# Three edits to a two-block layer stack on one core: an instruction of the second block tied to its place, parameter loads one step ahead, rotation tables later

## The chip, the cores and the metric

The kernel runs on one core of a Trainium2 chip. The metric is the device time of one execution in microseconds (us), the median over runs; the profile shows one execution, whose span (first to last instruction) is a little shorter than its time. Engines are named as the profile names them: PE (TensorE), DVE (VectorE), ACT (ScalarE), POOL (GpSimd) and SP (SyncE, which here only issues DMAs; SPq is its queue).

## The reference

Everything is float32, one sequence of 512 tokens of width 2048. Two blocks follow one another, each of two layers with adaptive modulation (shift, scale and gate from a vector c).

```python
def first_block(x, c, positions, ...):
    cos, sin = rope_tables(positions)
    for l in range(2):
        mod = silu(c) @ w_ada[l] + b_ada[l]          # shift, scale, gate
        h = rms_norm(x, norm_g[l]) * (1 + scale) + shift
        u, z, q, k, v = split(h @ w_in[l])
        y_ssm = s5_mixer(u, a, b, c, ...)            # state recurrence, 64 groups x 64 states
        y_att = diff_attention(rope(q), rope(k), v, lam)   # 8 heads, softmax - lam * softmax
        x = x + gate * (concat(y_ssm, y_att) * silu(z)) @ w_out[l]
    return rms_norm(x, final_g)

def second_block(x, c, ...):                         # gated delta rule beside sliding window attention
    beta = sigmoid(ba[..., 0:8])
    g = -exp(a_log) * softplus(ba[..., 8:16] + dt_bias)
    ...
```

## The kernel before

**Products.** Weights come from HBM as 128x1024 pieces. `piece()` (L255 to L272) loads one into a tile `raw` (L265, four buffers), ACT rounds it to `hi` (L266, three buffers), DVE writes the rest `lo = raw - hi` (L267, three buffers). Every product is made of three matmuls, hi with the rounded activations HH, hi with their rest HL, and lo with HH: L279, L280 and L282 for feature-major outputs (`mm3`), L352 to L354 for the token-major v. PE works through them in the order written.

**The ada weights** (w_ada) are streamed beside the rest: `ada_piece` loads one into a buffer of the same `raw` pool (L530) and DVE makes a dot product of it (L516). All loads go out on SP's queue, in order.

**Layers.** `layer` (L1011) runs the first block's two layers: the projections, then eight attention heads; beside these it takes steps of the state recurrence from the generator `ssm_steps` (L784). That prepares 64 chunk states in G, then runs 62 steps of three instructions on POOL (L812 to L814), written at a lower priority (`self.later(600)`). Each step multiplies by the table `A8[l]`. Then for eight groups it copies the states with four DMAs from G to a tile `s` (L830), each group's tile being one buffer, and multiplies them (L835, L837).

**The parameters** of the recurrence come from a generator `ssm_params` (L573), in quarters: `prep(qd)` loads a quarter of B and C (a DMA into a tile `rp`, three buffers) and makes their powers with DVE and POOL (L658 to L660). `par` is this generator for layer 0; `late()` in `build` takes its first step behind ssm_pad, rope_tables, lambdas and gain_root. rope_tables uses G's slots 0 to 3 as scratch; the first quarter uses 0 to 3 too.

**misc** is a tile of 128x640 with several uses: columns 0 to 127 hold A8 of layer 0, 128 to 255 that of layer 1, 384 to 511 the recurrence's scratch. In the second block `gates2` (L1138) takes 32-column slots of it by name; the fourth, `al`, is columns 96 to 127. `al` is written by one DVE instruction (L244) from `rep`, which holds a_log since the program's start.

**What sets the order.** The tile framework schedules the program itself. It takes the instructions by priority (the order in which they are written, unless changed) as soon as its own model sees their inputs and buffers ready, and so fixes one order for each engine and for each queue; the waits between engines follow from tiles read and written. An instruction whose inputs are there early can be placed far ahead of its neighbours in the source. At run time every engine takes its list strictly in order.

Of the kernel before, what the change touches and what calls it, by code (L numbers as in the profile page):

```python
# [11 lines left out]
I32 = mybir.dt.int32  # L12
# [156 lines left out]
class Kern:  # L169
# [282 lines left out]
    def rope_tables(self):  # L452
        nc = self.nc
        self.cosT, self.sinT = self.tab[:, :S], self.tab[:, S:]
        pi = self.G[:, 0, :].bitcast(I32)
        pf, r, w = (self.G[:, i, :] for i in (1, 2, 3))
        pos = self.I["pos"]
        nc.sync.dma_start(pi, bass.AP(tensor=pos.tensor, offset=pos.offset, ap=[[0, 128], [1, S]]))
        nc.vector.tensor_copy(pf, pi)
        self.ts(pf, pf, self.v("inv_freq"))  # L460
        self.reduce_angle(r, pf, w)
        lim = 3.1415925
        self.ts(r, r, -lim, lim, MAX, MIN)
        self.act(self.sinT, r, AF.Sin)
        self.ts(self.sinT, self.sinT, self.v("rope_sign"))
        self.act(w, r, AF.Sin, scale=0.5)
        self.tt(w, w, w, MUL)
        self.ts(self.cosT, w, -2.0, 1.0)
# [104 lines left out]
    def ssm_params(self, l):  # L573
# [5 lines left out]
        i = nc.sync.dma_start(ssa, I[f"ssa{l}"])  # L579
# [5 lines left out]
        def tmp(n, dt=F32):  # L585
            if n not in names:
                names[n] = cur[0]
                cur[0] += 32
            t = g[:, names[n]:names[n] + 32]
            return t if dt == F32 else t.bitcast(dt)  # L590
# [6 lines left out]
        step, x, th, e, em1, r, w2 = (tmp(k) for k in ("step", "x_", "th", "e", "em1", "rr", "w2"))  # L597
# [55 lines left out]
        def powmul(T, tm, out, f, src, n, qd, op=ADD):  # L653

            fv = f.rearrange("p (k r a) -> p k r a", k=2, r=2)[:, :, :, qd * 8:qd * 8 + 8]
            for r in range(2):
                t = tm[r][:, :8 * n].rearrange("p (a c) -> p a c", a=8)
                T(t, fv[:, 1, r].unsqueeze(2).to_broadcast([128, 8, n]), src[:, 1 - r], MUL)  # L658
                T(out[:, r], fv[:, 0, r].unsqueeze(2).to_broadcast([128, 8, n]), src[:, r], MUL)  # L659
                T(out[:, r], out[:, r], t, op)  # L660

        def prep(qd):
            sbq = self.t2("rp", 3).rearrange("p (k r a c) -> p k r a c", k=2, r=2, a=8)
            nc.sync.dma_start(sbq.rearrange("p k r a c -> p (k r) (a c)"),
                              I[f"ssb{l}"].rearrange("p (k q c) -> p k q c", k=4, q=4)[:, :, qd])
            tv = self.t2("n", 3), self.t2("n", 3)
            E = self.G[:, 4 * (qd % 2):4 * (qd % 2) + 4, :].rearrange("p a b -> p (a b)").rearrange("p (r a dc) -> p r a dc", r=2, a=8)
            powmul(V, tv, E[:, :, :, 0:16], cf, sbq[:, 0], 16, qd)
            for i, n in enumerate((16, 32, 64)):
                powmul(V, tv, E[:, :, :, n:2 * n], pw[i], E[:, :, :, 0:n], n, qd)  # L670

            nc.gpsimd.tensor_scalar(sbq[:, 1, 1], sbq[:, 1, 1], -1.0, None, MUL)

            Cb = self.t2("p", 4).rearrange("p (r a h c) -> p r a h c", r=2, a=8, h=2)
            nc.gpsimd.memset(Cb, 0.0)
            for h in range(2):
                rows = slice(64 * h, 64 * h + 64)
                nc.gpsimd.tensor_copy(Cb[rows, :, :, h, :], sbq[rows, 1])
            return E, Cb, sbq

        def products(E, Cb):
            kp = self.sbank("sc", 2)
            for x in range(2):
                for r in range(2):
                    for j in range(4):
                        a = 4 * x + j
                        nc.tensor.matmul(kp[32 * j:32 * j + 32, 128 * x:128 * x + 128], Cb[:, r, a].rearrange("p h c -> p (h c)"),
                                         E[:, r, a], start=r == 0, stop=r == 1)
            k2 = self.t2("p", 4)
            nc.scalar.copy(k2[:, :256], kp[:, :256])  # L690
            return kp, k2
# [18 lines left out]
        def turned(qd, E, rs):  # L710

            for r in rs:
                for a0 in range(0, 8, 4):
                    tp = self.sbank("tr", 2)
                    for a in range(4):
                        nc.tensor.transpose(tp[:, a * 128:(a + 1) * 128], E[:, r, a0 + a], self.ident)
                    ft = self.t2("p", 4)
                    nc.scalar.copy(ft, tp)
                    nc.sync.dma_start(self.FT_d[l][qd * 2 + a0 // 4, r], ft)

        def carried(qd, sbq):
# [7 lines left out]
            for r in range(2):  # L729
                for h in range(2):  # L730
                    nc.sync.dma_start(self.CA_d[l][qd][64 * r:64 * r + 64, h], CA[64 * h:64 * h + 64, r])
        made = prep(0)
        yield
        for qd in range(4):
            E, Cb, sbq = made
            k = products(E, Cb)
            turned(qd, E, (0,))
            yield
            turned(qd, E, (1,))
            lags(qd, *k)  # L740
            yield
            if qd < 3:
                made = prep(qd + 1)
            carried(qd, sbq)
            yield
            yield
# [394 lines left out]
    def gates2(self):  # L1141

        nc = self.nc
        ba = self.ba.rearrange("p (t c) -> p t c", c=16)
        used = {}

        def sm(name, dt=F32):
            i = used.setdefault(name, len(used))
            t = self.misc[:, 32 * i:32 * i + 32]
            return t if dt == F32 else t.bitcast(dt)  # L1150
        v3 = lambda t: t.rearrange("p (t h) -> p t h", h=8)
        x, e, y, al = sm("x"), sm("e"), sm("y"), sm("al")
        self.beta, self.nbeta, gc = sm("beta"), sm("nbeta"), sm("gc")

        self.ts(v3(x), ba[:, :, 0:8], -1.0)
        self.exp_acc(x, sm, e)
        self.ts(e, e, 1.0, None, ADD)
        nc.vector.reciprocal(self.beta, e)
        self.ts(self.nbeta, self.beta, -1.0)

        dt = self.rep[:, 8:16].unsqueeze(1).to_broadcast([128, 4, 8])
        self.tt(v3(x), ba[:, :, 8:16], dt, ADD)
        self.ts(y, x, -1.0)
        self.tt(y, y, x, MIN)
        self.exp_acc(y, sm, e)
        self.ts(y, e, 2.0, None, ADD)
        nc.vector.reciprocal(y, y)
        self.tt(e, e, y, MUL)
        self.tt(y, e, e, MUL)
        acc = sm("acc")  # L1170
        self.ts(acc, y, 2.0 / 17, 2.0 / 15)
        for k in (13, 11, 9, 7, 5, 3, 1):
            self.tt(acc, acc, y, MUL)
            self.ts(acc, acc, 2.0 / k, None, ADD)
        self.tt(acc, acc, e, MUL)
        self.stt(acc, x, 0.0, acc, MAX, ADD)
        self.ts(v3(al), self.rep[:, 0:8].unsqueeze(1).to_broadcast([128, 4, 8]), 1.0)
        self.exp_acc(al, sm, e)
        self.stt(acc, acc, -1.0, e, MUL, MUL)
        ps = self.sbank("sc", 2)  # L1180
        nc.tensor.matmul(ps[:, :32], self.tri, acc, start=True, stop=True)
        nc.vector.tensor_copy(gc, ps[:, :32])
        self.gc = gc

        ps = self.sbank("sc", 2)
        nc.tensor.transpose(ps[:32, :128], gc, self.ident)
        gt = self.t2("n", 3)[:32, :128]
        nc.vector.tensor_copy(gt, ps[:32, :128])
        self.g_d = self.dp.tile([32, 128], F32, name="g_d")
        nc.sync.dma_start(self.g_d, gt)  # L1190

        ps = self.sbank("sc", 2)
        nc.tensor.matmul(ps[:, :32], self.sellast, gc, start=True, stop=True)
        self.bg, self.kd, self.egl = sm("bg"), sm("kd"), self.misc[:, 512:544]
        assert len(used) <= 16
        self.exp_acc(gc, sm, self.bg)
        self.tt(self.bg, self.bg, self.beta, MUL)
        self.tt(x, ps[:, :32], gc, SUB)
        self.exp_acc(x, sm, self.kd)
        nc.vector.tensor_copy(e, ps[:, :32])  # L1200
        self.exp_acc(e, sm, self.egl)
# [403 lines left out]
def build(ctx, tc, I, O):  # L1605
    K = Kern(ctx, tc, I, O)
# [9 lines left out]
    for m in range(KT):  # L1616
        x, t = K.A[:, m, :], K.t2("n", 3)
# [11 lines left out]

    def late():  # L1630
        K.ssm_pad()
        K.rope_tables()
        K.lambdas()
        K.gain_root()
        next(par)
    K.start(K.acts(), before, late)
    xs = K.dp.tile([2, KT, 128, 512], F32, name="xs")


# [82 lines left out]
```

## Time and profile before

| | |
|---|---|
| runs shown | 3535.65, 3535.91, 3533.48 us |
| median | 3535.65 us |
| profiled execution | 3532.28 us |
| its span | 3530.5 us, mean granted TensorE clock 0.974 |
| PE busy | 3324.8 us (94% of the span) |
| DVE, ACT, POOL busy | 2190.3 (62%), 1217.0 (34%), 570.4 (16%) |
| DMA | 565.02 MB moved, mean 160 GB/s |

Shares are of the whole span; the stages differ. POOL is busy in two stretches only, once for each layer of the first block. A wait for several things is put down to the one that came last.

### The profile page before, as it was taken

Reading aid. Unit: us, or ns where it says so; the run is one execution under the profiler, and the core shown is the slowest. Engines: PE = TensorE matmul, PEld = TensorE weight load, DVE = VectorE, ACT = ScalarE, POOL = GpSimd, SP = SyncE. Lnnn points to the kernel's source line nnn. Section 1 sums busy time; section 2 is a strip of 40 time slices with the busy share of each in tenths; the row PEclk is TensorE's granted clock in tenths of the full one; section 3 lists DMA queues with packets and bytes.
Section 4 is the critical chain, followed back from the end, with each engine's and each line's share of the span. In section 5 each row is a group of like instructions: output and inputs, shape, how many; then the busy total and the mean of one; then the engine's idle time right before and its main releaser. Section 6 shows DMA issues by size and latency. Waiting matters only on the chain.

```text
span 3530.5 us, 45193 instructions
## 1 busy us (share of the span) xinstructions
PE 3324.8 (94%) x16541; PEld 2714.8 (77%) x16541; DVE 2190.3 (62%) x4244; ACT 1217.0 (34%) x2107; POOL 570.4 (16%) x732
## 2 busy tenths in 40 slices
PE   6988879999999888989999999999999999999999
PEld 4866657878888667777787887788888877788887
DVE  7993766767559736866665588933893266534432
ACT  3422433353233223333443344222532244433311
POOL 0073480000116605800001202000210000000000
PEclk8999989999999999999999999999999999999999
DMA  9857535757766775456567636333333332234442
GB/s 330 297 150 183 183 106 173 212 157 240 225 197 197 235 193 181 128 168 193 159 214 228 210 122 134 104 110 99 99 101 108 96 99 77 73 99 142 142 140 99
DMA packets 262813, 565.02 MB, mean 160 GB/s; under 512 B 74428, under 2 KB 111549, under 8 KB 262589
## 3 DMA queue, kind: packets, MB, share of 16 engines
q1 hardware_dynamic: 262590, 562.13, 52.2%
q8 instruction: 130, 2.13, 0.3%
q14 instruction: 93, 0.76, 0.1%
HBM read 497.89 MB, written 50.50 MB: 155 GB/s over the span
## 4 chain that ended last, share of the span: by engine, by line
PE 60%; DMA 12%; DVE 12%; POOL 8%; issue 4%; SPq 2%; ACT 2%; DVEq 0%; ACTq 0%; POOLq 0%
PE pp L280 17%; PE pp L279 17%; PE pp L282 17%; DMA raw<-in_wada 6%; DVE lo L267 3%; POOL misc L812 2%; DVE raw L516 2%; DMA raw<-in_win 2%; POOL G L814 2%; POOL misc L813 2%; DVE G L249 1%; POOL G L660 1%; DMA FT_d<-p 1%; POOL G L659 1%; DMA raw<-in_w 1%
## 5 line engine op out<-in xcount | busy, mean ns | idle before, releaser
L279 PE MATMUL pp<-HH,hi 128*128 128x512 f32 (+1 forms) x3568 | 1388.0, 392 | 40.5 <-ACT HH L566 20.7
L280 PE MATMUL pp<-HL,hi 128*128 128x512 f32 (+1 forms) x3440 | 1332.4, 391 | 1.5 <-DVE HL L252 1.5
L266 ACT CAST hi<-raw 128x1024 fp32r<-128x1024 f32 (+1 forms) x538 | 559.9, 1042 | 1142.9 <-PE pp L280 851.4
L282 PE MATMUL pp<-HH,lo 128*128 128x512 f32 (+1 forms) x3568 | 894.3, 388 | 0.1
L267 DVE TENSOR_TENSOR lo<-raw,hi 128x1024 fp32r<-128x1024 f32 (+1 forms) x538 | 668.9, 1245 | 359.2 <-PE pp L282 178.4
L279 PEld LDWEIGHTS pp<-HH,hi 128*128 128x128 f32 x3568 | 677.9, 190 | 184.2 <-ACT HH L566 22.3
L282 PEld LDWEIGHTS pp<-HH,lo 128*128 128x128 f32 x3568 | 656.8, 188 | 136.9 <-issue 6.3
L280 PEld LDWEIGHTS pp<-HL,hi 128*128 128x128 f32 x3440 | 653.0, 190 | 136.1 <-issue 7.0
L516 DVE CUSTOM_DVE_ANT_0 raw<-raw,cs,mod 128x1024 f32<-128x1024 f32 x112 | 148.2, 1324 | 235.4 <-DMA raw<-in_wada 235.2
L516 DVE CUSTOM_DVE_ANT_0 raw<-raw,cs,vec 128x1024 f32<-128x1024 f32 x112 | 151.6, 1353 | 167.3 <-DMA raw<-in_wada 167.1
L1676 POOL TENSOR_TENSOR rp<-rp,n 128x512 f32<-128x512 f32 (+1 forms) x43 | 59.9, 1406 | 994.1 <-ACT n L1675 581.4
L217 ACT ACTIVATE p<-p,st 128x128 f32<-128x128 f32 (+2 forms) x192 | 102.0, 531 | 258.1 <-DVE st L244 257.8
L812 POOL TENSOR_TENSOR misc<-misc,G 128x128 f32<-128x128 f32 x124 | 92.6, 747 | 237.9 <-ACT G L804 228.3
L352 PE MATMUL pp<-hi,HH 128*128 128x512 f32 (+1 forms) x320 | 121.9, 386 | 4.9 <-ACT HH L566 3.1
L353 PE MATMUL pp<-lo,HH 128*128 128x512 f32 (+1 forms) x320 | 120.7, 381 | 3.1 <-DVE lo L267 3.1
L354 PE MATMUL pp<-hi,HL 128*128 128x512 f32 (+1 forms) x320 | 116.1, 384 | 1.0 <-DVE HL L252 1.0
L280 PE MATMUL pp<-A,hi 128*128 128x512 f32 x256 | 100.7, 393 | 0.0
L660 POOL TENSOR_TENSOR G<-G,wt 128x128 f32<-128x128 f32 (+2 forms) x64 | 75.7, 1197 | 1.0
L217 ACT ACTIVATE n<-n 128x512 f32<-128x512 f32 x68 | 42.9, 631 | 94.2 <-DVE n L246 93.4
L352 PEld LDWEIGHTS pp<-hi,HH 128*128 128x128 f32 x320 | 62.5, 195 | 16.7 <-ACT HH L566 3.9
L936 PE MATMUL sc<-kh,q 128*128 128x128 f32 (+3 forms) x128 | 46.7, 367 | 28.2 <-DVE st L939 17.4
L814 POOL TENSOR_TENSOR G<-G,misc 128x64 f32<-128x64 f32 x124 | 71.2, 574 | 9.7
(332 smaller groups left out, 3924.6 us busy)
## 6 DMA issues: line engine op xcount, KB each, us to landing
raw<-in_wada SPq DMA_DIRECT2D x224, 512.0 KB, 4.1
raw<-in_w SPq DMA_DIRECT2D x164, 512.0 KB, 3.8
raw<-in_win SPq DMA_DIRECT2D x128, 512.0 KB, 4.6
raw<-in_wo SPq DMA_DIRECT2D x80, 512.0 KB, 4.6
G<-in_wad SPq DMA_DIRECT2D x64, 512.0 KB, 5.9
raw<-in_wv SPq DMA_DIRECT2D x32, 512.0 KB, 4.3
raw<-in_wglu SPq DMA_DIRECT2D x32, 512.0 KB, 4.4
raw<-in_wuA SPq DMA_DIRECT2D x18, 512.0 KB, 4.3
```

The lines of the kernel that those rows point to most:

```text
L217: i = self.nc.scalar.activation(out, src, func, **kw)
L266: nc.scalar.copy(hi[:, :n].bitcast(F32R), raw[:, :n])
L267: nc.vector.tensor_tensor(lo[:, :n].bitcast(F32R), raw[:, :n], hi[:, :n], SUB)
L279: mm(out, hi[:, sl], mh, start=first, stop=False)
L280: mm(out, hi[:, sl], ml, start=False, stop=False)
L282: mm(out, lo[:, sl], mh, start=False, stop=last)
L352: mm(pss[t][:, :n], mh[:, ts], hi[:, sl], start=first, stop=False)
L353: mm(pss[t][:, :n], mh[:, ts], lo[:, sl], start=False, stop=False)
L354: mm(pss[t][:, :n], ml[:, ts], hi[:, sl], start=False, stop=last)
L516: self.nc.vector.tensor_tensor_reduce(w, w, cs, 1.0, self.vec[:, o:o + 1] if first else m, MUL, ADD, m)
L812: T(s, a8, Sv[:, :, :, c - 1].unsqueeze(1).to_broadcast([128, 2, 2, 32]), MUL)
L814: T(Sv[:, :, :, c], Sv[:, :, :, c], s[:, 0], ADD)
```

## The change

It has three parts.

1. In `gates2`, `al` gets a tile of its own from the pool of `p` tiles (four buffers) instead of columns of `misc`.
2. In `ssm_params`, `prep(qd)` is split: `load(qd)` issues the DMA of B and C, `prep(qd, sbq)` does the rest, and the load of the next quarter is written ahead of the products of this one.
3. rope_tables, lambdas and gain_root are called after `K.start(...)`, in whose `late()` the first step of the parameters now stands alone; rope's scratch moves from G's slots 0 to 3 to slots 4 to 7.

```diff
@@ rope_tables
-        pi = self.G[:, 0, :].bitcast(I32)
-        pf, r, w = (self.G[:, i, :] for i in (1, 2, 3))
+        pi = self.G[:, 4, :].bitcast(I32)
+        pf, r, w = (self.G[:, i, :] for i in (5, 6, 7))
@@ ssm_params
-        def prep(qd):
+        def load(qd):
             sbq = self.t2("rp", 3).rearrange("p (k r a c) -> p k r a c", k=2, r=2, a=8)
             nc.sync.dma_start(sbq.rearrange("p k r a c -> p (k r) (a c)"),
                               I[f"ssb{l}"].rearrange("p (k q c) -> p k q c", k=4, q=4)[:, :, qd])
+            return sbq
+
+        def prep(qd, sbq):
             tv = self.t2("n", 3), self.t2("n", 3)
...
-        made = prep(0)
+        made = prep(0, load(0))
         yield
         for qd in range(4):
             E, Cb, sbq = made
+            if qd < 3:
+                after = load(qd + 1)
             k = products(E, Cb)
...
             if qd < 3:
-                made = prep(qd + 1)
+                made = prep(qd + 1, after)
             carried(qd, sbq)
@@ gates2
-        x, e, y, al = sm("x"), sm("e"), sm("y"), sm("al")
+        x, e, y, al = sm("x"), sm("e"), sm("y"), self.t2("p", 4)[:, :32]
@@ build
     def late():
         K.ssm_pad()
-        K.rope_tables()
-        K.lambdas()
-        K.gain_root()
         next(par)
     K.start(K.acts(), before, late)
+    K.rope_tables()
+    K.lambdas()
+    K.gain_root()
```

Below L661 the changed kernel's lines stand 3 to 5 higher (L830 becomes L835, L939 L944, L943 L948, L949 L954).

How the instructions move. First place, DVE in layer 0, the end of one attention head and the start of the next (st and p are softmax sums and probabilities, n a scaled output, raw and lo weight pieces). Before:

```order
794 L244 TENSOR_SCALAR st_3886<-st_3886 128x1 [waits DVE_49]
795 L943 RECIPROCAL st_3886<-st_3886 128x2 [waits Activation_49]
796 L244 TENSOR_SCALAR misc<-rep 128x32 [waits Pool_49]
797 L252 SCALAR_TENSOR_TENSOR st_341_3659<-st_341_3659 128x4 [waits DVE_49,Activation_49]
798 L249 TENSOR_TENSOR st_3886<-st_3886,neglam 128x1 [waits DVE_49]
799 L249 TENSOR_TENSOR st_341_3659<-st_341_3659 128x4 [waits DVE_49]
800 L244 TENSOR_SCALAR p_3897<-p_3897,st_3886 128x384 [waits DVE_49]
801 L516 ISA raw_4273,mod_100<-raw_4273,cs,mod_100 128x1024 [waits DMAHW4_49]
802 L516 ISA mod_100 128x1
803 L252 SCALAR_TENSOR_TENSOR st_341_3659<-st_341_3659 128x4 [waits DVE_49]
804 L252 SCALAR_TENSOR_TENSOR p_3890<-p_3890,st_3886,p_3897 128x384 [waits DVE_49]
805 L249 TENSOR_TENSOR n_3658<-tr_3647,st_341_3659 128x512 [waits DVE_49]
```

In the changed kernel the row `misc<-rep` is gone from here. What stood behind it comes in much the same sequence up to n_3658, and further on:

```order
809 L252 SCALAR_TENSOR_TENSOR st_341_3659<-st_341_3659 128x4 [waits DVE_49]
810 L249 TENSOR_TENSOR n_3658<-tr_3647,st_341_3659 128x512 [waits DVE_49]
811 L516 ISA raw_4321,mod_100<-raw_4321,cs,mod_100 128x1024 [waits DMAHW2_49]
812 L516 ISA mod_100 128x1
813 L267 TENSOR_TENSOR lo_4239<-raw_4237,hi_4238 128x1024 [waits Activation_49]
814 L252 SCALAR_TENSOR_TENSOR A_86<-tr_3671,subg,A_86 128x512 [waits PE_49]
815 L944 ISA p_3923,st_3912<-sc_3920,cst 128x512 [waits PE_49]
816 L944 ISA st_3912 128x1
817 L244 TENSOR_SCALAR st_3912<-st_3912 128x1 [waits DVE_49]
818 L516 ISA raw_4393,mod_100<-raw_4393,cs,mod_100 128x1024 [waits DMAHW4_49]
819 L516 ISA mod_100 128x1
820 L267 TENSOR_TENSOR lo_4269<-raw_4267,hi_4268 128x1024 [waits DMAHW3_49,Activation_49]
```

The two L516 on ada weights stand on this side of lo_4239 and lo_4269; before, L516 of raw_4393 stood behind p_3916, one row after its last write.

Second place, SP's queue at the end of layer 0's recurrence (G_90 holds the states), in the changed kernel:

```order
308 L265 DMA raw_4315<-in_win 128x1024 [waits DMAHW5_49,DVE_49]
309 L835 DMA s_412_4357<-G_90 64x256 [waits Pool_49]
310 L835 DMA s_412_4357<-G_90 64x256 [waits DMAHW7_49]
311 L835 DMA s_412_4357<-G_90 64x256 [waits DMAHW0_49]
312 L835 DMA s_412_4357<-G_90 64x256 [waits DMAHW1_49]
313 L530 DMA raw_4321<-in_wada 128x1024 [waits DMAHW2_49,DVE_49]
314 L265 DMA raw_4387<-in_win 128x1024 [waits DMAHW3_49,DVE_49]
315 L530 DMA raw_4393<-in_wada 128x1024 [waits DMAHW4_49,DVE_49]
316 L265 DMA raw_4568<-in_win 128x1024 [waits DMAHW5_49,DVE_49]
```

Before, the same nine rows stand two rows higher in the same sequence (L830 for L835): nothing moved.

Third place, PE in the changed kernel, weight piece raw_4237 and the transposes of p_3916:

```order
1533 L279 MATMUL pp_4236<-HH,hi_4238 128x512 [waits Activation_49]
1534 L280 MATMUL pp_4236<-HL,hi_4238 128x512
1535 L279 MATMUL pp_4236<-HH,hi_4238 128x512
1536 L280 MATMUL pp_4236<-HL,hi_4238 128x512
1537 L279 MATMUL pp_4236<-HH,hi_4238 128x512
1538 L280 MATMUL pp_4236<-HL,hi_4238 128x512
1539 L279 MATMUL pp_4236<-HH,hi_4238 128x512
1540 L280 MATMUL pp_4236<-HL,hi_4238 128x512
1541 L279 MATMUL pp_4236<-HH,hi_4238 128x512
1542 L954 MATMUL tr_3931<-cst,p_3916 128x128 [waits DVE_49]
1543 L954 MATMUL tr_3931<-cst,p_3916 128x128 x3
1544 L280 MATMUL pp_4236<-HL,hi_4238 128x512
```

Before, these transposes (L949) stood amid the products of the piece ahead of this one, ten rows higher; now nine products on this piece stand ahead of them.

## Rows read from the trace of the kernel before

**Rows 1.** Waits of PE, whole span: who waited for what, us in total, times, longest

```profile
PE tr L967 <- DVE n L249: 20.8, 3, 19.2
```

**Rows 2.** PE's timeline: start us, us, operation, shape, count, [idle before <-releaser]

```profile
505.11 0.39 PE L352 MATMUL pp<-hi,HH 128*128 128x512 f32 x1
505.33 0.39 PE L353 MATMUL pp<-lo,HH 128*128 128x512 f32 x1
524.90 1.09 PE L967 MATMUL tr<-cst,n 128*128 128x128 f32 x4 [19.18 <-DVE n L249]
...
538.37 0.60 PE L949 MATMUL tr<-cst,p 128*128 128x128 f32 x4
...
560.24 0.44 PE L835 MATMUL sc<-A,G 128*64 128x128 f32 x4
```

**Rows 3.** DVE's timeline of the same stretch

```profile
521.33 0.18 DVE L244 TENSOR_SCALAR misc<-rep 128x32 f32<-128x32 f32 x1 [22.35 <-POOL misc L812]
...
530.88 1.28 DVE L516 CUSTOM_DVE_ANT_0 raw<-raw,cs,mod 128x1024 f32<-128x1024 f32 x1 [4.32 <-DMA raw<-in_wada]
...
533.36 1.22 DVE L267 TENSOR_TENSOR lo<-raw,hi 128x1024 fp32r<-128x1024 f32 x1
...
535.52 0.17 DVE L943 RECIPROCAL st<-st 128x2 f32<-128x2 f32 x1 [0.88 <-ACT p L217]
...
536.52 0.74 DVE L252 SCALAR_TENSOR_TENSOR p<-p,st,p 128x512 f32<-128x512 f32 x1
...
538.63 1.28 DVE L516 CUSTOM_DVE_ANT_0 raw<-raw,cs,mod 128x1024 f32<-128x1024 f32 x1 [1.36 <-DMA raw<-in_wada]
```

**Rows 4.** POOL's timeline: first step of layer 0's recurrence, step 47, its end

```profile
399.11 0.65 POOL L812 TENSOR_TENSOR misc<-misc,G 128x128 f32<-128x128 f32 x1 [93.36 <-ACT G L804]
...
499.29 0.52 POOL L812 TENSOR_TENSOR misc<-misc,G 128x128 f32<-128x128 f32 x1
...
521.77 0.36 POOL L814 TENSOR_TENSOR G<-G,misc 128x64 f32<-128x64 f32 x1
```

**Rows 5.** SP's queue (SPq): the DMA issues of the same stretch

```profile
523.57 0.33 SPq L265 DMA_DIRECT2D raw<-in_win  x1
523.95 2.44 SPq L830 DMA_DIRECT2D s<-G  x4
526.52 0.49 SPq L530 DMA_DIRECT2D raw<-in_wada  x1
...
534.61 0.33 SPq L530 DMA_DIRECT2D raw<-in_wada  x1
```

**Rows 6.** Windows: us, busy PE, PEld, DVE, ACT, POOL (x), PEclk, DMA share, GB/s

```profile
399.00:499.00 100.00, 92.25 (x443) 74.27 (x443) 86.04 (x199) 41.75 (x116) 89.16 (x138) 0.98 0.54 164
499.00:521.00 22.00, 6.72 (x30) 5.21 (x28) 0.00 (x0) 1.05 (x1) 18.40 (x47) 0.71 0.02 9
505.00:525.00 20.00, 0.82 (x5) 0.39 (x4) 3.67 (x11) 0.00 (x0) 14.32 (x36) 0.58 0.01 3
525.00:530.00 5.00, 5.00 (x17) 4.18 (x18) 1.56 (x4) 2.01 (x4) 0.00 (x0) 0.63 0.94 254
```

**Rows 7.** Timelines of POOL, SP, DVE and PE, end of layer 1's recurrence

```profile
1496.26 0.36 POOL L814 TENSOR_TENSOR G<-G,misc 128x64 f32<-128x64 f32 x1
...
1496.65 2.43 SPq L830 DMA_DIRECT2D s<-G  x4
...
1502.93 1.28 DVE L516 CUSTOM_DVE_ANT_0 raw<-raw,cs,vec 128x1024 f32<-128x1024 f32 x1 [9.85 <-DMA raw<-in_wada]
...
1505.97 0.80 PE L936 MATMUL sc<-kh,q 128*128 128x512 f32 x1 [7.27 <-DVE st L939]
```

**Rows 8.** PE's timeline, parameter stage of layer 0

```profile
194.60 0.76 PE L279 MATMUL pp<-HH,hi 128*128 128x512 f32 x1 [5.70 <-DVE n L658]
...
234.06 1.94 PE L716 MATMUL tr<-cst,G 128*128 128x128 f32 x8 [7.17 <-issue]
```

**Rows 9.** PE's timeline, the second block near gates2

```profile
2160.19 2.03 PE L1248 MATMUL sc<-G 128*128 128x128 f32 x8 [4.17 <-DVE G L249]
```


## The prediction

> **What bounds the kernel now.** I read the table of shares first: TensorE (PE) is busy 94% of the span, so only the places where PE waits can give time back. The list of waits, sorted by total, puts one wait on top [rows 1]: PE for a VectorE (DVE) result at L249, three times, one of them 19.2 us, the longest of the kernel. The timeline of PE shows where it lies [rows 2]: PE issues its last product at 505.33, stands 19.18 us and goes on at 524.90. DVE's timeline names the cause [rows 3]: the write `misc<-rep` (L244, 128x32, 0.18 us) waited 22.35 us for L812 on GpSimd (POOL). That is the write of `al` in `gates2`, an instruction of the second block which has been moved into layer 0; its 32 columns of `misc` lie in the table that the 62-step recurrence reads, so it may only run when the recurrence has read the table for the last time. POOL's timeline gives the recurrence [rows 4]: 399.11 to 521.77 + 0.36 = 522.13. All that DVE has behind that write, the n that PE needs included, stands still.
>
> Last I read the queue of SyncE (SP), since it feeds PE with weights [rows 5]. A load can only go out when its buffer is free, so SP too stood behind DVE until 523.57. Right behind that load are the four copies `s<-G`, which read what the recurrence wrote last, and all later loads follow them in the same queue.
>
> **Part 1, al leaves misc.** In the changed order (first place) DVE loses the early wait: 22.35 us of DVE and, by the plain reading, 19.18 us of PE. The granted clock was 0.58 on average in 505 to 525 and 0.63 in 525 to 530 [rows 6]: PE had been idle, fell from 2.4 to 1.2 GHz, and stayed there for a good part of its first busy stretch, so that after the restart 5 x 0.37 = 1.9 us of work was lost. So the most this part can give is 19.2 + 1.9 = 21.1 us.
>
> I do not think that it gives it. SP's order is unchanged (second place): the first `s<-G` waits for Pool, and raw_4321 (the ada weights), raw_4387 and raw_4393 are queued behind it. DVE has L516 of raw_4321 at its row 811 and L516 of raw_4393 at its row 818, both ahead of p_3916, on which PE's transposes tr_3931 wait (third place). So the wait on the recurrence goes from DVE's write to SP's copies, and I follow it from there.
>
> *What PE has in hand.* Counted in the changed order from the point where PE stopped: 4 products left of one weight piece, 24, 24, and 9 of the next before tr_3931, in all 61, and 10 transposes. Products are 505.33 - 505.11 = 0.22 to 0.23 us apart [rows 2], four transposes take 0.60 us, so 61 x 0.23 + 10 x 0.15 = 15.5 us. PE runs dry at 505.5 + 15.5 = 521.0 instead of 505.7.
>
> *When the recurrence ends.* While DVE was 86% busy (399 to 499) 46 steps took 499.29 - 399.11 = 100.2 us, 2.18 us each; with DVE idle (499 to 521, busy 0.00) the last 16 took 22.84 us, 1.43 each [rows 4, 6]. The 46 x 0.75 = 34.5 us of delay over 86 us of DVE work is 0.40 us for each us. Now DVE does, beside these 16 steps, what it did before only after its wait, 3.67 + 1.56 = 5.2 us between 505 and 530 [rows 6]. Estimate: 5.2 x 0.40 = 2.1 us later, 524.2. Ends: nothing, if the DVE work falls between POOL's instructions, and 16 x 0.75 = 12 us, if all 16 steps run at 2.18.
>
> The row shows that POOL's steps are slower while DVE works, and by how much. The Trainium skill (SBUF — State Buffer, "SBUF: two separate sides") gives a reason: DVE and GpSimd share a pair of ports as an exclusive lock, and whoever comes second waits for the other's whole instruction, when DVE reads two SBUF inputs or runs in a two-port mode. By that rule the 5.2 us could delay POOL by up to 5.2 us and not 2.1, and the sum below would be 3.1 us higher. The trace agrees with the direction; no row separates the forms.
>
> *From there to PE.* From rows 5 and 3: the copies take 526.52 - 523.95 = 2.57 us to the next issue: 526.8. From that issue to L516 on the ada weights 530.88 - 526.52 = 4.36: 531.2. L516 1.2: 532.4. lo_4239 (L267) 1.2: 533.6; that frees the buffer for raw_4393, which before went out at 534.61, just after the same L267. From its issue to its L516 538.63 - 534.61 = 4.02: 537.6. L516 1.2 and lo_4269 1.2: 540.0. The four instructions from L943 to the end of p_3916, 535.52 to 537.26, 1.7: 541.7. PE thus waits from 521.0 to 541.7, 20.7 us, for 19.2 before.
>
> *What is left after that.* Before, PE took 560.24 - 538.37 = 21.87 us from tr_3931 to the first L835 [rows 2], with 78 products; now 63 are left, 15 x 0.23 = 3.4 less: 18.4. The restart costs its 1.9 us at the half clock as before. 541.7 + 18.4 + 1.9 = 562.0, against 560.24: **+1.8 us**, with -0.3 if POOL is not slowed.
>
> Layer 1 has no such write, and shows the same queue at work already [rows 7]: the recurrence ended at 1496.62, the copies went out at 1496.65, DVE's L516 behind them waited 9.85 us for the ada load, and PE 7.27 us. That is the second price for this place.
>
> **Part 2, loads one step ahead.** In the order neither the first layer nor the second moves a load by more than a place in SP's queue: they stood early before. I cost it at nothing; below nothing is excluded for the same reason.
>
> **Part 3, rotation tables behind the first quarter.** No work is added; the rope instructions come some 8 rows later on DVE, and the reads that free PE's accumulator banks slip a few rows behind parameter work: PE's wait of 5.70 us at 194.60 [rows 8] gets longer, at most twice as long. I take zero, because the next wait, 7.17 us at 234.06, hangs on the parameter chain, whose rows keep their places, and takes up what PE loses before it. Ends: -3 and +5.7.
>
> **Second block.** The write of al, 0.18 us, is now done there, and some DVE rows of `gates2` come about 16 places later; DVE is not the bound there. PE's wait of 4.17 us at 2160.19 [rows 9] could double. I take zero, ends 0 and +4.2.
>
> **Sum.** +1.8 + 0 + 0 + 0 = +1.8 us. The profiled execution took 3532.28, 3.4 under the median of 3535.65; a difference carries over, so against the median 3537.4.
>
> **Rivals.**
> - *The new wait costs what it costs in layer 1.* PE pays 7.27 us instead of 19.18, and about the same clock: -12, so 3523.7. For it: same code, same queue. Against it: in layer 1 only one load lay between the copies and PE's operand, here two with two L516. Chance 0.24.
> - *The stall falls away whole*: -21.1, 3514.5. It needs loads that don't wait for the recurrence, or a recurrence that ends over 15 us earlier; the order shows neither. Chance 0.10.
> - *Slower: the recurrence is dragged out.* With DVE freed, the last 16 steps run at 2.18 us like the first 46, the copies and all loads come 12 us later instead of 2.1: +11.7, 3547.4. It decides from about 13 us of DVE work beside those steps; I count 5.2, but the rows behind it may slip in, and part 3's slip would add to it. The skill's port rule above pulls the same way. Chance 0.20.
> - *The change doesn't do what it says*: the early loads move nothing, which is already in the sum.
>
> **How the numbers follow.** The forecast, the stall moved and not removed, gets 0.46, with its own range 3531 to 3543 (-0.3 to +1.8, and about 5 us either way for parts 3 and the second block). The full range must leave out at most 0.2: it takes in layer 1's price with 3 us below and the dragged recurrence, and leaves out the whole gain: 3520 to 3548. Within 0.2% (7 us, about what a measurement of this kernel can tell from no change) lies the forecast: 0.46. Faster: the first two rivals, 0.34. Slower: 0.20.
>
> **What would show it.** Right, if DVE's wait before L244 is gone, PE's 19 us wait ends later (near 520 to 540) and is put down to p (L252) or an ada load, SP's first `s<-G` goes out at the recurrence's end, 522 to 526, and L516 behind it waits for DMA. The step on POOL is right if the last 16 steps take 24 to 26 us. Wrong, if PE has no wait over 8 us between 500 and 560, or if the waits between 190 and 300 differ by more than 5 us in sum.

## The result and the profile after

| | before | after |
|---|---|---|
| median | 3535.52 us (4 runs) | 3558.07 us (4 runs, 3553.67 to 3565.03) |
| ratio | 1 | 1.0063 [1.0051, 1.0075] |
| profiled execution, its span | 3532.28, 3530.5 us | 3557.99, 3556.2 us |
| mean granted clock | 0.974 | 0.970 |
| PE, DVE busy | 3324.8, 2190.3 us | 3336.7, 2200.5 us |

The change makes the kernel 22.5 us slower, outside the range of 3520 to 3548; the forecast was 3537.4. Of the span's 25.7 us, 11.9 are PE's busy time for the same 16541 instructions, at a lower clock, and 13.8 are idle time of PE.

To see where they arise I set the two traces side by side by PE's products: the time between the k-th and the m-th product of one is subtracted from that of the other, with k and m at the times of the trace of before that head the columns. (The lists are equally long.) All kernels of the study but the three with K_d on POOL's queue stand here; the runs behind the first two rows are of the same kernel.

| us against before's profile | 5–219 | 219–452 | 452–565 | 565–636 | 636–764 | 764–2122 | 2122–2951 | sum to the end |
|---|---|---|---|---|---|---|---|---|
| the change | 4.5 | 1.9 | −2.2 | 0.7 | 8.2 | 1.8 | 10.5 | 25.3 |
| the change again (e5_after) | 5.7 | −1.4 | −0.5 | 2.1 | 3.5 | −3.6 | 8.3 | 12.1 |
| part 1 alone (e2_al) | −0.4 | 2.1 | 1.3 | −0.5 | −0.3 | −5.7 | 7.2 | 5.2 |
| al in free columns of misc (e1_own) | 1.7 | 1.6 | 2.6 | 0.2 | 2.7 | 0.2 | −1.3 | 5.8 |
| al in y's columns (e9_al_y) | 1.0 | 2.6 | 1.7 | −0.1 | 1.6 | −0.4 | −0.8 | 5.3 |
| part 3 alone (e3_rope) | 4.4 | 2.0 | −1.6 | −0.1 | 10.8 | 2.4 | −3.4 | 14.0 |
| part 3 again (e17_rope) | 3.5 | 0.9 | −0.6 | −0.4 | 10.7 | 2.3 | 0.5 | 16.3 |
| part 3, scratch slots 7 to 4 (e16_rope_perm) | 3.7 | 2.0 | 2.3 | −1.6 | 1.6 | −3.4 | −2.3 | 0.5 |
| slots 4 to 7 alone (e6_slots) | 2.5 | 2.2 | 0.7 | −0.8 | 5.9 | 3.2 | −0.6 | 12.5 |
| later calls alone (e7_calls) | 14.6 | −0.1 | 0.9 | −1.5 | 2.2 | −0.9 | −0.2 | 14.5 |
| e1_own and part 3 (e8_own_rope) | 4.7 | 0.9 | −2.2 | −0.3 | 12.9 | −1.8 | −0.8 | 11.5 |
| e1_own, all `s` copies on POOL's queue (e4_own_poolq) | 2.6 | 4.9 | −21.2 | 3.3 | 7.4 | −10.1 | −3.4 | −16.3 |
| e1_own, first group's copies there (e10_own_pool0) | 0.6 | 1.3 | −21.8 | 3.8 | 9.0 | −7.7 | −0.5 | −15.7 |
| e9_al_y, all `s` copies there (e11_y_pool) | 0.5 | 2.3 | −21.0 | 2.7 | 10.0 | −6.3 | −2.0 | −15.1 |
| the change, all `s` copies there (e12_after_pool) | 3.4 | 0.6 | −20.1 | −0.1 | 2.7 | −7.2 | 7.2 | −13.8 |

These are single executions, and a row's sum can stand several us from the ratio of its medians; a stretch is read only where several kernels agree. They agree on this: the place the prediction was about, 452 to 565, is even where the copies stay on SP's queue; the loss lies ahead of 452, in 636 to 764, and in the second block. The edge at 219 cuts through a loss that is made up again: counted from 5 us, the eight kernels with part 3 or with its slots (e7_calls aside) stand 2.5 to 5.7 us behind at 219, between 2.2 ahead and 0.3 behind at 320, and 4.0 to 6.5 behind at 452. The three kernels with al alone stand 1.7 to 3.6 behind at 452.

**The place of the forecast.** PE's list of waits after, by total (who waited for what, us, times, longest):

```profile
PE pp L279 <- ACT HH L566: 20.6, 3, 10.0
PE tr L954 <- DVE A L252: 18.8, 3, 17.6
PE sc L941 <- DVE st L944: 18.2, 11, 8.7
```

The wait for n [rows 1] is gone and another of nearly its length stands there. PE's timeline, then DVE's, SP's and POOL's of the changed kernel (columns as in [rows 2]):

```profile
520.70 0.38 PE L954 MATMUL tr<-cst,p 128*128 128x128 f32 x2
538.68 0.90 PE L954 MATMUL tr<-cst,p 128*128 128x128 f32 x3 [17.60 <-DVE A L252]
```

```profile
535.53 1.28 DVE L516 CUSTOM_DVE_ANT_0 raw<-raw,cs,mod 128x1024 f32<-128x1024 f32 x1 [20.68 <-DMA raw<-in_wada]
...
537.88 0.75 DVE L252 SCALAR_TENSOR_TENSOR A<-tr,subg,A 128x512 f32<-128x512 f32 x1
```

```profile
506.12 0.33 SPq L265 DMA_DIRECT2D raw<-in_win  x1
529.24 2.43 SPq L835 DMA_DIRECT2D s<-G  x4
531.77 0.53 SPq L530 DMA_DIRECT2D raw<-in_wada  x1
```

```profile
404.63 0.72 POOL L817 TENSOR_TENSOR misc<-misc,G 128x128 f32<-128x128 f32 x1 [99.51 <-ACT G L809]
...
504.00 0.54 POOL L817 TENSOR_TENSOR misc<-misc,G 128x128 f32<-128x128 f32 x1
...
528.85 0.36 POOL L819 TENSOR_TENSOR G<-G,misc 128x64 f32<-128x64 f32 x1
```

DVE's 22.35 us behind the write of al [rows 3] have become 20.68 us behind an ada load. SP issues nothing from 506.12 to 529.24: the copies at the head of its queue wait for the recurrence, which ends at 528.85 + 0.36 = 529.21, and the ada load goes out behind them. PE loses 17.60 us for 19.18.

**636 to 764.** PE's waits there, by the trace after; before had one wait of 6.2 us for DVE instead:

```profile
PE sc L842 <- DMA s<-G: 4.9, 3, 2.3
PE sc L840 <- DMA A<-K_d: 3.7, 1, 3.7
```

```profile
PE tr L967 <- DVE G L842: 6.2, 1, 6.2
```

The windows of the same products, after and then before (columns as in [rows 6]), show 9.9 us of idle time for 6.2, and 4.8 us more of busy time at a lower clock:

```profile
640.93:777.38 136.45, 126.54 (x703) 103.67 (x702) 90.67 (x241) 47.57 (x132) 0.00 (x0) 0.95 0.61 174
```

```profile
636.27:764.24 127.97, 121.74 (x702) 99.67 (x700) 90.54 (x242) 47.76 (x132) 0.00 (x0) 0.97 0.66 188
```

**The second block.** PE's timeline and POOL's after, then POOL's before:

```profile
2185.01 0.80 PE L1131 MATMUL tr<-wt,ones 128*128 128x512 f32 x1 [4.83 <-POOL wt L1129]
```

```profile
2176.99 3.11 POOL L1249 TENSOR_TENSOR G<-G,cst 128x512 f32<-128x512 f32 x1 [1.80 <-ACT G L217]
2180.05 3.16 POOL L1250 TENSOR_TENSOR A<-A,cst 128x512 f32<-128x512 f32 x1
2183.17 1.79 POOL L1129 TENSOR_TENSOR wt<-n,wt 128x512 fp32r<-128x512 f32 x1
```

```profile
2148.63 1.66 POOL L1245 TENSOR_TENSOR A<-A,cst 128x512 f32<-128x512 f32 x1 [1.35 <-ACT A L217]
2150.25 1.28 POOL L1124 TENSOR_TENSOR wt<-n,wt 128x512 fp32r<-128x512 f32 x1
2151.49 1.30 POOL L1244 TENSOR_TENSOR G<-G,cst 128x512 f32<-128x512 f32 x1
```

Before, POOL made wt ahead of the last pair on G and A, and PE waited 0.92 us for it; now wt stands behind that pair, whose two instructions take 3.1 us each, and PE waits 4.83. This wait is not the whole loss. PE's waits here, from the list after and then from that before:

```profile
PE tr L1133 <- ACT n L1123: 7.3, 2, 3.8
PE tr L1131 <- POOL wt L1129: 7.0, 2, 4.8
...
PE sc L1253 <- DVE G L249: 0.3, 1, 0.3
```

```profile
PE tr L1128 <- ACT n L1118: 3.8, 1, 3.8
...
PE tr L1126 <- POOL wt L1124: 0.9, 1, 0.9
```

PE now waits twice for wt and twice for n, while the wait of 4.17 us for G [rows 9] is gone. Between 2122 and 2334 this makes 3.9 us more idle time and 2.6 us more busy time; the second wait for n, near 2883, adds 3.5. POOL does not stand idle in the second block, as the remark on its two busy stretches may suggest: between 2122 and 2334 it is busy for 28.0 us before and for 37.1 us after.

### The profile page after: what moved, and what is told of

Same layout as the page of the kernel before. It is cut to its first block, busy times and chain, and to the rows that moved or that the text cites. A ratio compares the mean times of both kernels' runs of the same rounds, so it can differ in the third digit from the quotient of the medians.

```text
span 3556.2 us, 45179 instructions
## 1 busy us (share of the span) xinstructions
PE 3336.7 (94%) x16541; PEld 2722.1 (77%) x16541; DVE 2200.5 (62%) x4244; ACT 1217.4 (34%) x2107; POOL 573.1 (16%) x732
## 5 line engine op out<-in xcount | busy, mean ns | idle before, releaser
L279 PE MATMUL pp<-HH,hi 128*128 128x512 f32 (+1 forms) x3568 | 1392.5, 394 | 45.9 <-ACT HH L566 20.6
L516 DVE CUSTOM_DVE_ANT_0 raw<-raw,cs,mod 128x1024 f32<-128x1024 f32 x112 | 147.4, 1316 | 258.8 <-DMA raw<-in_wada 258.7
L516 DVE CUSTOM_DVE_ANT_0 raw<-raw,cs,vec 128x1024 f32<-128x1024 f32 x112 | 150.0, 1339 | 157.2 <-DMA raw<-in_wada 156.9
L352 PE MATMUL pp<-hi,HH 128*128 128x512 f32 (+1 forms) x320 | 122.3, 387 | 14.6 <-DVE A L249 11.5
L353 PEld LDWEIGHTS pp<-lo,HH 128*128 128x128 f32 x320 | 62.6, 196 | 13.0 <-DVE lo L267 3.2
```

What stands on the lines that cost most here:

```text
L279: mm(out, hi[:, sl], mh, start=first, stop=False)
L352: mm(pss[t][:, :n], mh[:, ts], hi[:, sl], start=first, stop=False)
L353: mm(pss[t][:, :n], mh[:, ts], lo[:, sl], start=False, stop=False)
L516: self.nc.vector.tensor_tensor_reduce(w, w, cs, 1.0, self.vec[:, o:o + 1] if first else m, MUL, ADD, m)
```

## The experiments

### Where al lies: e1_own, e2_al, e9_al_y

```diff
-        x, e, y, al = sm("x"), sm("e"), sm("y"), sm("al")
+        ... al = columns 544:576 of misc, which are free      # e1_own
+        ... al = self.t2("p", 4)[:, :32]                      # e2_al, part 1 alone
+        ... al = y's columns                                  # e9_al_y
```

> Kernel before with one edit: al lies in 32 free columns of misc (544 to 575) that no other step reads, so DVE writes it at the start of the program and waits for nothing; all else is ordered as before. Theory 1 (the wait of layer 0 passes from DVE to the copies s<-G in SP's queue, and costs PE the same): 3533 to 3539 us, a wait of PE of 15 to 21 us that begins near 519 to 521. Theory 2 (the freed DVE drags out the recurrence, and that is the loss of the changed kernel): 3543 to 3550. Plain reading (the wait goes away): 3513 to 3517.

> Kernel before with part 1 alone, as the change has it (al in a p tile, written in the second block). The order differs from before in layer 0 by the one row, and in the second block in some thousand rows. Theory 1 (loss by rows that moved): as the run with al in free columns up to 2150 us, then 7 to 11 us lost in the second block, 3541 to 3549. Theory 2 (loss in layer 0): slower by 8 to 13 before 600 us, nothing in the second block. If the second block's loss belongs to parts 2 or 3: 3533 to 3539.

> Part 1 done another way: al written over y, which gates2 has read for the last time just before; tied to its place, but no p tile is held. Only 112 rows on DVE stand otherwise than before; PE, ACT, POOL and SP are ordered as before. Theory 1 (the second block's loss, some 9 us between 2122 and 2951, comes of the order that the held p tile makes): none of it, 3532 to 3539, as al in free columns. Rival (writing al late costs there by itself): 4 us or more lost between 2122 and 2334.

Measured: e1_own 1.0012 [0.9999, 1.0024], e2_al 1.0019 [1.0009, 1.0029], e9_al_y 0.9998 [0.9987, 1.001]. In all three the wait on the recurrence is there, on the same transposes as after the change (PE's timelines of e1_own, e2_al and e9_al_y):

```profile
537.55 0.90 PE L949 MATMUL tr<-cst,p 128*128 128x128 f32 x3 [22.72 <-DVE A L252]
```

```profile
535.41 0.90 PE L949 MATMUL tr<-cst,p 128*128 128x128 f32 x3 [21.26 <-DVE A L252]
```

```profile
536.94 0.90 PE L949 MATMUL tr<-cst,p 128*128 128x128 f32 x3 [23.35 <-DVE A L252]
```

These waits are longer than the 15 to 21 us expected of e1_own, whose wait begins at 514.8 and not at 519 to 521. So freeing the write of al gives nothing, whichever way it is done: the stretch 452 to 565 comes out 1.3 to 2.6 us longer. In the second block only the kernels with al in a `p` tile lose: e2_al, e12_after_pool and both runs of the change 7.2 to 10.5 us, all others −3.4 to 0.5. The traces agree: with the buffer taken from the pool the framework draws another order for the second block (in e2_al 2513 of PE's 16541 instructions differ from those of before at the same place, all but 12 of them behind 2100 us), while in e9_al_y only DVE's order differs, PE's nowhere, and nothing is lost. The two waits on wt, 7.0 us with 4.8 the longer, stand in e2_al too.

### The copies off SP's queue: e4_own_poolq, e10_own_pool0, e11_y_pool, e12_after_pool

```diff
-   self.after(nc.sync.dma_start(s2[...], Sv[...]), self.raw_dma)
+   nc.gpsimd.dma_start(s2[...], Sv[...])       # e10_own_pool0: in the first of eight groups only
```

e4_own_poolq and e10_own_pool0 have al as e1_own, e11_y_pool as e9_al_y; e12_after_pool is the whole change.

> al in free columns, and the copies s<-G are issued from POOL's queue instead of SP's, so that weight loads do not stand behind the recurrence. Theory 1: PE's wait near 520 falls under 5 us, 3514 to 3522 us, if POOL's issues cost nothing elsewhere. Rival (PE's wait hangs on something else that ends with the recurrence, or issues from POOL are slow): a wait of 10 us or more stays, 3528 or more.

> al in free columns; of each layer's eight groups only the first issues its copies s<-G from POOL's queue, the others from SP's as before. Theory 1 (it is the first group, behind the recurrence, that holds the loads): as with all groups on POOL's queue, 3510 to 3522. If the other groups' copies matter more: 3525 or more.

> al over y, and all copies s<-G from POOL's queue: a kernel that should beat both. Theory 1: 3510 to 3520. If the tie costs something: 3521 to 3530.

> The changed kernel with all copies s<-G from POOL's queue. If what parts 1 and 3 lose elsewhere (first stage +4, second block +8 us) stays and the wait at the recurrence's end goes: 3522 to 3535, no better than before by more than 10. If their losses hang on SP's queue: 3510 to 3520.

Measured: 0.9944 [0.9931, 0.9957], 0.9956 [0.9943, 0.997], 0.9954 [0.9937, 0.9971], and 0.9976 [0.996, 0.9992] for the change. SP's queue, POOL's timeline and the window of the last 16 steps of e4_own_poolq:

```profile
504.22 0.33 SPq L530 DMA_DIRECT2D raw<-in_wada  x1
510.26 0.33 SPq L265 DMA_DIRECT2D raw<-in_win  x1
513.33 0.33 SPq L530 DMA_DIRECT2D raw<-in_wada  x1
518.31 0.33 SPq L265 DMA_DIRECT2D raw<-in_win  x1
520.71 0.33 SPq L530 DMA_DIRECT2D raw<-in_wada  x1
```

```profile
536.95 0.36 POOL L814 TENSOR_TENSOR G<-G,misc 128x64 f32<-128x64 f32 x1
537.63 1.77 POOL L830 DMA_DIRECT2D s<-G  x3 [0.32 <-POOL G L814]
542.85 0.53 POOL L830 DMA_DIRECT2D s<-G  x1 [3.45 <-issue]
```

```profile
505.50:537.30 31.80, 31.80 (x158) 26.43 (x157) 18.66 (x43) 12.31 (x33) 28.04 (x49) 1.00 0.48 141
```

SP now feeds PE throughout, PE is busy in every one of the 31.8 us at the full clock, and that stretch is 20 to 22 us shorter in all four kernels. This is the forecast's ceiling of 21.1 us, reached with both waits taken away, DVE's by moving al and SP's by moving the copies. Moving al alone gave nothing; moving the copies alone was not run (that DVE's write would then still hold the n that PE needs is argued, not shown). The copies of one group in each layer suffice (e10_own_pool0). It also carries out the third rival: with DVE at work, the last 16 steps take 31.7 us instead of 22.84, and PE does not wait for them in this stretch. In layer 1 PE's wait of 7.27 us [rows 7] is gone too (its longest wait for st there is 1.4 to 1.9 us in all four), which is part of the 6.3 to 10.1 us that they gain between 764 and 2122.

The Trainium skill (DMA: Bandwidth & Descriptors, "Issuing engines are not separate DMA queues") says that starting DMAs from several engines saves only the issuing time, which is usually small. Here the issuing engine's list also held the loads behind a copy that waited; the measurement decides, 20 us in this stretch.

Part of it is given back in 636 to 764 in the first three (7 to 10 us; PE waits there for these copies, K_d or CA_d), less in e12_after_pool.

### Part 3 and its halves: e3_rope, e17_rope, e6_slots, e7_calls, e8_own_rope, e16_rope_perm

```diff
-        pi = self.G[:, 0, :].bitcast(I32)                # e3, e6, e8, e17: slots 4, 5, 6, 7
-        pf, r, w = (self.G[:, i, :] for i in (1, 2, 3))  # e16: 7, 6, 5, 4;  e7: as before
...
-        K.rope_tables(); K.lambdas(); K.gain_root()      # e3, e7, e8, e16, e17: behind K.start(...)
```

e7_calls changes the computation: rope's scratch overwrites the powers of the first quarter.

> Kernel before with part 3 alone (tables behind the first quarter); al waits in layer 0 as before. Rows on DVE, ACT, PE and SP move in layer 0 only. Theory 1: 5 to 14 us lost between 190 and 760 us, outside the recurrence's end, none later; 3541 to 3550. Theory 2: no change beyond 0.1%, 3532 to 3539.

> Half of part 3: rope's scratch in slots 4 to 7 of G, the calls where they were; al waits in layer 0. Its order is nearly that of the whole of part 3 (57 rows on DVE differ). Theory 1 (layer 0 loses by the order that this makes, 565 to 780 us): as part 3 alone, 3540 to 3548, with the PE waits for s<-G and for A<-K_d near 670 and 735. Rival (the loss comes of the late calls): 3533 to 3538.

> The other half of part 3: the three calls behind the first quarter of parameters, the scratch in slots 0 to 3. Another order (527 rows on DVE). Theory 1 (the loss is that of one particular order): without the waits near 670 and 735, 3530 to 3540. Rival (late calls cost by themselves): 3540 to 3548.

> al in free columns, and part 3: the changed kernel's layer 0, with the second block ordered as before. If the changed kernel's loss is the sum of layer 0 (parts 1 and 3) and 4 to 9 us in the second block: 3543 to 3550, and the second block as before within 1 us. If the second block loses nothing by part 1: as the changed kernel.

> Part 3 alone, with its scratch in the same four slots of G the other way round (7, 6, 5, 4). The scheduler then draws an order that has 15 products between the last two groups in layer 0, as before, not 9. Theory 1 (the loss between 636 and 764 us is that of the order drawn): under 3 us there; the first stage still loses 2 to 6 us before 219; 3533 to 3541. Rival (part 3's rows cost there whatever the order): 6 us or more there, 3540 to 3548.

> Part 3 alone as the change has it, once more, beside the run with the slots reversed. Theory 1: 3538 to 3548, 6 to 13 us lost between 636 and 764, and slower than that run by 3 to 9 us.

Measured: e3_rope 1.0022 [1.001, 1.0034], e17_rope (the same kernel) 1.0029 [1.0018, 1.004], e6_slots 1.0035 [1.0023, 1.0048], e7_calls 1.003 [1.0017, 1.0042], e8_own_rope 1.0025 [1.0009, 1.0041], e16_rope_perm 1.0004 [0.9992, 1.0016].

The stretch 636 to 764 sorts them. I counted, in PE's instruction lists, the 128x512 products between the output groups of layer 0 (L835): between the last two of the eight groups stand 15 before, in e1_own, e2_al, e9_al_y, e7_calls and e16_rope_perm, and these lose −0.3 to 2.7 us; 9 stand there in the change, e3_rope, e17_rope, e6_slots and e8_own_rope, and these lose 3.5 to 12.9. The count marks an order and is no price by itself: in e4_own_poolq and e11_y_pool 16 stand there, and these lose 7.4 and 10.0. PE's waits in the stretch and the window, of e3_rope and then of e16_rope_perm:

```profile
PE sc L837 <- DMA s<-G: 5.0, 2, 3.6
PE sc L835 <- DMA A<-K_d: 4.4, 1, 4.4
```

```profile
640.29:779.36 139.07, 129.34 (x702) 105.75 (x701) 91.09 (x243) 47.73 (x132) 0.00 (x0) 0.93 0.59 170
677.40:700.00 22.60, 22.60 (x111) 18.24 (x112) 13.88 (x40) 6.40 (x25) 0.00 (x0) 0.81 0.66 194
700.00:734.50 34.50, 32.80 (x196) 26.08 (x194) 21.85 (x58) 13.03 (x38) 0.00 (x0) 1.00 0.62 178
738.90:760.00 21.10, 21.03 (x111) 17.56 (x112) 11.98 (x41) 7.58 (x22) 0.00 (x0) 0.79 0.42 126
```

```profile
PE tr L967 <- DVE G L842: 3.7, 1, 3.7
```

```profile
642.03:771.84 129.81, 124.99 (x702) 101.85 (x700) 91.86 (x247) 48.02 (x133) 0.00 (x0) 0.96 0.64 187
```

e3_rope and e16_rope_perm contain the same edit; only the numbers of the four scratch slots are turned round, and the framework draws another order from it. So the loss belongs to the order drawn and not to the later tables. Of e3_rope's 139.07 − 127.97 = 11.1 us, 3.5 are idle time (9.7 for 6.2) and 7.6 are busy time (129.34 − 121.74): PE stands 3.60 us ahead of 677.40 and 4.35 us ahead of 738.9, and in the 20 us behind each the clock averages 0.81 and 0.79, so part of both ran at 1.2 and not 2.4 GHz. What in this order makes the transfers late, the six products of cover (6 x 0.23 = 1.4 us, less than the wait) or the places in SP's queue, is not settled.

Up to 219 any form of part 3 that keeps the computation loses 2.5 to 5.7 us, e16_rope_perm included (e7_calls 14.6), and the kernels with al alone −0.4 to 1.7. The wait of 5.70 us [rows 8] has grown, and the next one, 7.17 us, has shrunk, in PE's timeline after:

```profile
196.91 0.77 PE L279 MATMUL pp<-HH,hi 128*128 128x512 f32 x1 [8.29 <-DVE G L660]
...
235.40 0.85 PE L719 MATMUL tr<-cst,G 128*128 128x128 f32 x6 [3.91 <-ACT p L721]
```

By 320 all of this loss has been made up. Between 320 and 452 the same eight kernels lose 4.5 to 6.9 us, and the other six of the table −0.3 to 3.1. PE's idle time there is 20.6 us after and 15.3 before, in several waits of up to 4 us; what makes them is not settled.

### K_d on POOL's queue: e13_y_pool_kd, e14_al_y_kd, e15_rope_kd

These were to tell whether the copies `A<-K_d` lose by their place in SP's queue: e11_y_pool, e9_al_y and e3_rope with

```diff
-   nc.sync.dma_start(tz[16 * d:16 * d + 16]..., src)       # L825, A<-K_d, eight for each group
+   nc.gpsimd.dma_start(tz[16 * d:16 * d + 16]..., src)
```

> The kernel with al over y and the copies s<-G on POOL's queue, with the copies A<-K_d on POOL's queue too. That kernel lost 7 to 10 us against before between 636 and 764 us; if PE's waits for A<-K_d and A<-CA_d behind weight loads are the cause: 3505 to 3514 us. If POOL's issues become the new wait: 3518 to 3530.

> al over y, with only the copies A<-K_d on POOL's queue; s<-G stays on SP's, so PE's wait near 520 stays. Theory 1: 3526 to 3536 us; between 636 and 764 within 4 us of before. Rival (issues from POOL are slow): 3540 or more.

> Part 3 alone, with the copies A<-K_d on POOL's queue; al waits in layer 0. If the place of A<-K_d in SP's queue makes part 3's loss of 6 to 13 us between 636 and 764: under 4 us there against the run without part 3, 3530 to 3539 us in all. If not: 6 us or more there, 3538 to 3546.

All failed: 1.0511 [1.0497, 1.0526], 1.049 [1.0475, 1.0504], 1.0505 [1.0484, 1.0526]. PE's waits of e14_al_y_kd, and POOL's timeline of e15_rope_kd:

```profile
PE sc L835 <- DMA A<-K_d: 163.0, 12, 21.5
```

```profile
559.44 0.55 POOL L825 DMA_DIRECT2D A<-K_d  x1 [3.70 <-issue]
564.16 0.53 POOL L825 DMA_DIRECT2D A<-K_d  x1 [4.18 <-issue]
569.56 0.54 POOL L825 DMA_DIRECT2D A<-K_d  x1 [4.86 <-issue]
```

A copy from POOL goes out every 3 to 5 us for the most part, where SP issues eight in about 4 us; the new price hides the question, which stays open.

### The change once more: e5_after

> The changed kernel once more, in more rounds, beside the runs it is to be compared with. If parts 1 and 3 simply add (part 1 alone +7, part 3 alone +8 us): 3548 to 3554. If they make each other worse, as the first four runs had it: 3555 to 3562.

Measured 1.0061 [1.0047, 1.0074], as in the first runs (1.0063). Parts 1 and 3 alone give 0.0019 + 0.0022 to 0.0029 = 0.0041 to 0.0048. The 0.0013 to 0.0022 that remain, 5 to 8 us, are about as large as the intervals of the three together; whether the parts add up is not resolved. Part 2 was not run alone: with al in a `p` tile, the instruction lists of all five engines are the same with it and without it.

## Why the prediction was wrong

**Part 1, the wait moves: right.** DVE's early wait is gone, the `s` copies go out at the recurrence's end, and L516 behind them waits for its load, as the text asked. They went out at 529.24, past the 522 to 526 named, since the recurrence began 5.5 us later than before; and PE's wait is put down to A (L252), neither to p nor to an ada load. The last 16 steps took 529.21 − 504.00 = 25.2 us, 2.4 more than before for a forecast of 2.1, inside 24 to 26; part of this is luck, since DVE worked 8.8 us beside them and not 5.2, at 0.27 us of delay for each and not 0.40. The stretch came out at −2.2 and −0.5 us in the two profiles of the change and at 1.3 to 2.6 in e1_own, e2_al and e9_al_y, for +1.8.

Two of its steps were off and cancelled, which is luck too. Counted from step 47 of the recurrence, PE was to stop 521.0 − 499.29 = 21.7 us later and to go on after 541.7 − 499.29 = 42.4; it stopped after 521.1 − 504.00 = 17.1 and went on after 538.68 − 504.00 = 34.7. I let PE run to tr_3931, behind two L516 on ada loads. It stopped at a transpose that needs the bank freed by `A<-tr` (L252), row 814 of the DVE list shown: fewer products in hand, and only one L516 ahead.

**Part 2 at nothing: right**, by the lists.

**Part 3 at nothing: this step failed, behind the place that it looked at.** There it held: the wait at 194.60 grew from 5.70 to 8.29 us, less than twofold, the next one shrank from 7.17 to 3.91, PE's waits between 190 and 300 came to 25.0 us for 23.5, and by 320 the loss was made up. But I priced only the stage in which the moved instructions stand. Two terms were missing. Between 320 and 452 the change lost 6.3 us in the first profile and 4.9 in the second, with the cause open. Some 450 us behind the moved instructions the order of layer 0's output groups was drawn anew: 8.2 us in the first profile and 3.5 in the second, 10.8 and 10.7 with part 3 alone.

**The second block at nothing: this step failed.** I saw "some DVE rows about 16 places later" and doubled one wait of 4.17 us. That wait went away. The loss, 10.5 and 8.3 us, comes of another order there: 6.1 us more for POOL's wt, which now stands behind two instructions of 3.1 us, and 3.5 more for n. It comes from where al was put, not from taking al out of the recurrence's table.

**The sum.** By stretches the first profile gives 6.4 (up to 452) − 2.2 (the stall) + 8.2 (output groups) + 10.5 (second block) + 2.5 (elsewhere, within what the other kernels show) = 25.4.

**The rivals.** Layer 1's price and the whole gain fell: the stretch was even. The slower rival had the sign but not the cause: the last 16 steps were not dragged to 35 us. In e4_own_poolq they were, to 31.7, and the kernel was faster. Nor could 13 us of DVE work have done it: at the text's own 0.40 they give 5 us, and the 12 us ask for 30. The range reached to 3548 since it held only known places; an edit that redraws the order of two later stages should have had a bound there.

On the port: DVE worked 8.8 us beside these steps after the change and cost POOL 2.4 us, in e2_al 4.4 us and cost 2.3, in e4_own_poolq 18.7 us and cost 8.9, so 0.27, 0.51 and 0.48 us for each us, around the 0.40 from [rows 4, 6]. By the rule that I set beside it (the Trainium skill, SBUF — State Buffer, "SBUF: two separate sides") the cost could be the whole of DVE's time; these runs show about half at most.

## What to carry to other kernels

When a wait is taken off one engine, look for the in-order queue that holds the same dependency. Here al's move gave nothing until the waiting copies, too, went to a queue with nothing urgent behind them; the two together brought the stall's 20 us, and those versions without parts 2 and 3 (0.9944 to 0.9956) beat both kernels. Where a framework draws the order, a new tile or a renumbered slot is an edit to every later stage that shares its pool: compare the instruction lists of all stages, and price each place where the cover of a transfer or the turn of a slow engine has moved. For a 32-column temporary, free columns of a tile left nearly the whole order alone and a pool buffer did not.

## What the runs showed of the hardware

- A copy can cost POOL's queue far more than SP's, by its shape: the four `s` copies of a group took 2.7 to 6.4 us on POOL (e4_own_poolq, e11_y_pool, e12_after_pool) and mostly 2.5 on SP; the eight K_d copies, 16 partitions each, are mostly 3 to 5 us apart on POOL and about 0.5 on SP.
- Short waits of PE can cost more than themselves: in e3_rope 3.60 and 4.35 us of idle time were followed by a clock of about 0.8 in the next 20 us, and in that stretch PE's busy time grew by 7.6 us, twice the added idle time (3.5 us). The length of the wait alone does not set this: before, the 20 us behind a wait of 6.16 us, at 726.46, ran at 0.91.
